# Solving the triangular inverse from the last row upwards, in a stick-breaking and RWKV-7 block on one core

## The chip, the core and the metric

The kernel runs on one core of a Trainium2 chip. Its metric is the device time of one execution in microseconds (us). Before the change the median of three runs is 1595.77 us (1595.27 to 1598.77). In this text PE is the matrix engine, PEld its weight loads, DVE the vector engine, ACT the scalar engine, POOL the general-purpose engine and SP the engine that issues the transfers.

## The reference

One block of a network on x of 1024 tokens by 1024 channels, float32: a normalised input projection, two parallel branches (causal stick-breaking attention with 8 heads, and RWKV-7 time mixing with 8 heads of 64 channels), a gated merge, an output projection and a gated feed-forward part. The change touches the RWKV-7 branch alone, whose core is a recurrence over the tokens:

```python
def step(state, inp):
    r_t, w_t, k_t, v_t, kk_t, a_t = inp
    sa = jnp.einsum('bhvk,bhk->bhv', state, -kk_t)
    state = (state * w_t[:, :, None, :]
             + sa[..., None] * (kk_t * a_t)[:, :, None, :]
             + v_t[..., None] * k_t[:, :, None, :])
    return state, jnp.einsum('bhvk,bhk->bhv', state, r_t)
```

The kernel computes it in chunks of 64 tokens. Within a chunk the steps depend on each other through a strictly triangular 64x64 matrix N per head and chunk, and the chunk's result needs the inverse of (I - N).

## The kernel before

**The order of the work.** The kernel first records every operation with its engine, and then a planner (`Block.schedule`, L413) puts all of them in an order: it simulates the engines with a cost for each operation (`cost`, L131), latencies between engines (L247) and a priority, and gives out the SBUF and PSUM places on the way. The operations are then issued in that order, so each engine works through a fixed queue. A recorded operation has the same line in the profile (L585), whoever recorded it; groups are told apart by the names of their tiles. The planner's price of a vector product depends on how its first operand is read: L155 gives `68 + 1.8 * n` ns if the last step of that operand is over 16 elements, and L157 gives `68 + 1.042 * n` otherwise, with n elements per partition.

**The stages.** Normalisation and small projections; the RWKV-7 branch (`rwkv`, L867); attention (L1130); merge; output projection; feed-forward. The RWKV-7 branch has four pairs of heads and two halves of the sequence, so eight units. A unit is one call of `rw_elementwise` (L896), which makes the chunk matrices `nx` (tile b_nx) and calls `rw_inverse` (L1024); afterwards `rw_chain` (L1075) carries the state through the eight chunks (tiles b_xv, b_sv) and `rw_post` finishes. Projections of the next pair and of the gates (tiles d_d, big_h) are recorded as fillers, which the planner lays between the steps of these units.

**The inverse.** A unit has 16 matrices of 64x64 (8 chunks by 2 heads). Each is cut in 32x32 blocks. Their two diagonal blocks are inverted by substitution on DVE, 32 blocks side by side; the block below is then made with two groups of small matmuls. The steps are:

1. `nd`: the diagonal blocks go to DRAM, and from there come back as `nl` (b_nl, L1029): 128 partitions, each with a whole 32x32 block, four partitions for one block. POOL writes the ones on the diagonal (L1030).
2. The substitution (L1035 to L1038): 31 steps, each of one product and one reduction. Step t multiplies column t of the block, read down the rows with a step of 32 elements, with the t+1 entries found so far of n rows of the inverse, and sums each product into one entry. The block is broadcast over the n rows.
3. Four stores to DRAM (`td`) and one load bring the inverse with its rows on partitions (`dt`, L1047). DVE transposes 32x32 blocks of it (`dn`, L1051).
4. `dn` is copied to `tt` by POOL (L1054) and is the right operand of the first group of small matmuls (`ph`, L1063); `dt` is the weight of the second (`pt`, L1069), which also needs two DVE copies of `ph`.

The tiles ts, tm, dt, dn and hb are all of the class q (four places), so they show as q_q.

Of the kernel before, what the change touches and what calls it, by code (L numbers as in the profile page):

```python
# [10 lines left out]
ALU = mybir.AluOpType  # L11
AX = mybir.AxisListType
# [3 lines left out]
P = 128  # L16
# [879 lines left out]
def rw_elementwise(b, u, p, hf, spill):  # L896
# [108 lines left out]
    with Offset(b, INV):  # L1005
        tt = rw_inverse(b, nd, nx, quads, tinit, p, hf)


        for g in range(2):
            pt = T("y", [P, 4, P])  # L1010
            cs = slice(4 * g, 4 * g + 4)
            with b.together():
                for c in range(4):
                    for h, rs in enumerate(halves):
                        nc.tensor.matmul(pt[rs, c, 0:CH], lhsT=tt[rs, 4 * g + c, :], rhs=bkt[rs, 4 * g + c, rs], start=True, stop=True)
                    for h, rs in enumerate(halves):
                        nc.tensor.matmul(pt[rs, c, CH:P], lhsT=tt[rs, 4 * g + c, :], rhs=nx[g][rs, c, 1, h, :], start=True, stop=True)
            for h, rs in enumerate(halves):
                nc.scalar.copy(bkt[rs, cs, rs], pt[rs, :, 0:CH])
                nc.scalar.copy(nx[g][rs, :, 1, h, :], pt[rs, :, CH:P])  # L1020
                nc.scalar.copy(nx[g][rs, :, 0, h, :], ar[rs, cs, 0:CH])


def rw_inverse(b, nd, nx, quads, tinit, p, hf):  # L1024

    nc = b.nc
    T = b.t
    nl = T("b", [P, 8 * P], F32, "nl")
    nc.sync.dma_start(nl[:], nd.rearrange("c a s t -> (c a) (s t)")[:, None, :].broadcast_to([32, 4, 1024]))  # L1029
    nc.gpsimd.memset(nl[:, 0:1024:33], 1.0)  # L1030
    nl = nl.rearrange("l (s t) -> l s t", s=32)
    ts = T("q", [P, 8, 32])
    nc.sync.dma_start(ts[:], tinit.rearrange("l (j t) -> l j t", j=8))
    tm = T("q", [P, 8, 32])
    for t in range(1, 32):  # L1035
        n = (t + 3) // 4
        nc.vector.tensor_tensor(out=tm[:, :n, : t + 1], in0=nl[:, None, 0 : t + 1, t].broadcast_to([P, n, t + 1]), in1=ts[:, :n, : t + 1], op=ALU.mult)
        nc.vector.tensor_reduce(out=ts[:, :n, t], in_=tm[:, :n, : t + 1], axis=AX.X, op=ALU.add)  # L1038
    td = b.scratch([32, 8, 4, 32], f"td{p}{hf}")
    stores = set()  # L1040
    for c in range(4):

        nc.sync.dma_start(td[:, :, c, :], ts[c:P:4])
        b.ops[-1].preds -= stores
        stores.add(b.ops[-1])
    dt = T("q", [P, 8, 32])
    nc.sync.dma_start(dt[:], td.rearrange("(c a) j k t -> (a j k) c t", a=4))  # L1047
    b.ops[-1].late = SHORT_RUNS

    dn = T("q", [P, 8, 32])  # L1050
    nc.vector.transpose(out=dn.rearrange("p c t -> p (c t)"), in_=dt.rearrange("p c t -> p (c t)"))  # L1051
    tt = T("b", [P, 8, CH], F32, "tt")
    for h, q, rs, qs in quads:
        nc.gpsimd.tensor_copy(tt[rs, :, qs], dn[rs])  # L1054
        if q == 0:
            nc.gpsimd.memset(tt[rs, :, 32:CH], 0.0)
    ph = T("y", [P, 8, 32])
    hb = T("q", [P, 8, 32])
    top = [slice(0, 32), slice(CH, CH + 32)]
    bot = [slice(32, CH), slice(CH + 32, P)]  # L1060
    with b.together():
        for c, h in ((c, h) for c in range(8) for h in range(2)):
            nc.tensor.matmul(ph[bot[h], c, :], lhsT=nx[c // 4][top[h], c % 4, 0, h, 32:CH], rhs=dn[top[h], c, :], start=True, stop=True)  # L1063
    for h in range(2):
        nc.vector.tensor_copy(hb[bot[h]], ph[bot[h]])
    pt = T("y", [P, 8, 32])
    with b.together():
        for c, h in ((c, h) for c in range(8) for h in range(2)):
            nc.tensor.matmul(pt[bot[h], c, :], lhsT=dt[bot[h], c, :], rhs=hb[bot[h], c, :], start=True, stop=True)  # L1069
    for h in range(2):  # L1070
        nc.scalar.copy(tt[bot[h], :, 0:32], pt[bot[h]])
    return tt
# [680 lines left out]
```

## Time and profile before

| what | value |
|---|---|
| median of the timed runs | 1595.77 us (1595.27 to 1598.77, 3 runs) |
| span of the profiled execution | 1597.4 us, 23915 instructions |
| DVE, ACT, POOL busy over the span | 1176.4, 733.4, 205.0 us |
| substitution's products and reductions | from 125.5 to 468 us, 248 of each |
| mean granted PE clock | 0.997 |
| transfers | 180.38 MB, mean 113 GB/s |

The profile records one execution. For each engine it lists when it worked, what it waited for when it did not, and in which queue position; the span is from the first instruction to the last. A row of a group gives the number of instructions, their total time in us and the mean of one in ns, and behind it how long the engine stood idle just before them.

### The profile page before, as it was taken

Reading aid. Unit: us, or ns where it says so; the run is one execution under the profiler, and the core shown is the slowest. Engines: PE = TensorE matmul, PEld = TensorE weight load, DVE = VectorE, ACT = ScalarE, POOL = GpSimd, SP = SyncE. Lnnn points to the kernel's source line nnn. Section 1 sums busy time; section 2 is a strip of 40 time slices with the busy share of each in tenths; the row PEclk is TensorE's granted clock in tenths of the full one; section 3 lists DMA queues with packets and bytes.
Section 4 is the critical chain, followed back from the end, with each engine's and each line's share of the span. In section 5 each row is a group of like instructions: output and inputs, shape, how many; then the busy total and the mean of one; then the engine's idle time right before and its main releaser. Section 6 shows DMA issues by size and latency. Waiting matters only on the chain.

```text
span 1597.4 us, 23915 instructions
## 1 busy us (share of the span) xinstructions
PE 1573.5 (99%) x8884; PEld 1275.1 (80%) x8884; DVE 1176.4 (74%) x2104; ACT 733.4 (46%) x1445; POOL 205.0 (13%) x383
## 2 busy tenths in 40 slices
PE   9999999999999999999999999999999999999998
PEld 7877877777778888888788888888888888888876
DVE  7568779878884888896269799766666666877585
ACT  7533334444345666675445664332332333454352
POOL 1031233433323232230000000000000000000000
PEclk9999999999999999999999999999999999999999
DMA  6523332342321000103643531232233233964445
GB/s 218 202 77 88 100 104 57 84 136 78 106 80 35 33 28 14 41 21 106 198 138 106 170 121 73 99 113 99 86 112 99 95 117 125 317 230 138 144 147 184
DMA packets 106822, 180.38 MB, mean 113 GB/s; under 512 B 42321, under 2 KB 43345, under 8 KB 106706
## 3 DMA queue, kind: packets, MB, share of 16 engines
q1 hardware_dynamic: 106706, 178.85, 34.3%
q8 instruction: 70, 1.15, 0.3%
q14 instruction: 46, 0.38, 0.1%
HBM read 129.27 MB, written 47.45 MB: 111 GB/s over the span
## 4 chain that ended last, share of the span: by engine, by line
PE 88%; DVE 6%; DMA 3%; ACT 1%; issue 1%; POOL 0%; SPq 0%; DVEq 0%; ACTq 0%; POOLq 0%
PE d_d L585 42%; PE e_e L585 19%; PE c_c L585 16%; PE y_y L585 12%; DVE q_q L585 1%; DMA b_wraw<-w_fd 1%; DVE big_h L585 0%; DVE b_nx L585 0%; DVE b_sv L585 0%; DVE b_xs L585 0%; DVE b_wraw L585 0%; DMA b_mg<-gsc 0%; DVE b_wd L585 0%; DMA b_tmp<-cum_d 0%; DMA g_d<-b_sg 0%
## 5 line engine op out<-in xcount | busy, mean ns | idle before, releaser
L585 PE MATMUL d_d<-big_h,whi_whi 128*128 128x512 f32 x1312 | 440.2, 408 | 1.6 <-ACT b_tmp L585 1.6
L585 PEld LDWEIGHTS d_d<-big_h,whi_whi 128*128 128x128 f32 x1312 | 240.7, 189 | 50.9 <-issue 5.0
L585 PE MATMUL d_d<-big_h,wlo_wlo 128*128 128x512 f32 x656 | 268.6, 410 | 0.0
L585 PEld LDWEIGHTS d_d<-big_h,wlo_wlo 128*128 128x128 f32 x656 | 123.9, 189 | 25.3 <-issue 2.9
L585 DVE TENSOR_TENSOR q_q<-b_nl,q_q 128x2 f32<-128x2 f32 (+30 forms) x248 | 88.3, 356 | 20.0 <-PE y_y L585 8.0
L585 ACT CAST whi_whi<-raw_raw 128x1024 fp32r<-128x1024 f32 (+1 forms) x58 | 53.7, 928 | 88.6 <-PE d_d L585 80.9
L585 DVE TENSOR_TENSOR_SCAN b_nb<-b_nb 128x128 f32<-128x128 f32 (+3 forms) x64 | 85.2, 1351 | 2.2 <-POOL b_nb L585 1.8
L585 DVE TENSOR_TENSOR wlo_wlo<-raw_raw,whi_whi 128x1024 fp32r<-128x1024 f32 (+1 forms) x58 | 63.3, 1092 | 26.1 <-ACT whi_whi L585 20.0
L585 POOL TENSOR_SCALAR sp_sp<-b_sv,pl_pl 64x64 f32<-64x64 f32 x120 | 61.3, 511 | 133.6 <-DVE b_sv L585 127.8
L585 ACT CAST b_wd<-b_wraw 128x512 fp32r<-128x512 f32 x70 | 42.3, 620 | 66.5 <-DVE b_wraw L585 31.5
L585 DVE TENSOR_REDUCE q_q<-q_q 128x1 f32<-128x2 f32 (+30 forms) x248 | 62.0, 250 | 6.8
L585 PE MATMUL e_e<-b_wd,big_act 128*128 128x512 f32 x264 | 66.5, 394 | 0.0
L585 PE MATMUL d_d<-b_wd,big_act 128*128 128x512 f32 x264 | 66.5, 394 | 0.0
L585 DVE TENSOR_TENSOR b_wd<-b_wraw,b_wd 128x512 fp32r<-128x512 f32 x70 | 46.5, 686 | 26.4 <-ACT b_wd L585 26.2
L585 PEld LDWEIGHTS e_e<-b_wd,big_act 128*128 128x128 f32 x264 | 49.6, 188 | 11.7
L585 PEld LDWEIGHTS d_d<-b_wd,big_act 128*128 128x128 f32 x264 | 49.6, 188 | 11.7
L585 POOL TENSOR_SCALAR_AFFINE_SELECT b_nb<-b_nb 128x128 f32<-128x128 f32 x64 | 40.1, 632 | 123.1 <-ACT b_nb L585 121.8
L585 DVE TENSOR_TENSOR b_wt<-c_c,b_wt 128x512 fp32r<-128x512 f32 (+2 forms) x96 | 50.4, 547 | 2.1 <-ACT b_wt L585 0.9
L585 PE MATMUL y_y<-b_wd,big_act 128*128 128x512 f32 x198 | 50.7, 394 | 0.9 <-DVE b_u L585 0.9
L585 PE MATMUL c_c<-b_wd,big_act 128*128 128x512 f32 x198 | 50.7, 394 | 0.2 <-DVE b_wd L585 0.2
L585 ACT COPY b_xv<-c_c 64x64 f32<-64x64 f32 x64 | 13.3, 208 | 79.0 <-PE c_c L585 44.4
L585 ACT CAST b_wt<-c_c 128x512 fp32r<-128x512 f32 (+2 forms) x96 | 43.6, 481 | 11.9 <-PE c_c L585 10.8
(635 smaller groups left out, 3536.0 us busy)
## 6 DMA issues: line engine op xcount, KB each, us to landing
raw_raw<-w_in SPq DMA_DIRECT2D x42, 512.0 KB, 3.6
act<-b_u SPq DMA_DIRECT2D x46, 256.0 KB, 2.3
raw_raw<-w_fg SPq DMA_DIRECT2D x22, 512.0 KB, 3.5
raw_raw<-w_fu SPq DMA_DIRECT2D x22, 512.0 KB, 3.6
b_wraw<-w_fd SPq DMA_DIRECT2D x22, 512.0 KB, 6.0
b_x<-x SPq DMA_DIRECT2D x16, 512.0 KB, 5.5
b_mg<-gsc SPq DMA_DIRECT2D x28, 256.0 KB, 5.4
raw_araw<-act SPq DMA_DIRECT2D x14, 512.0 KB, 6.3
```

Source lines behind the costliest of these rows:

```text
L585: getattr(getattr(self.real, op.engine), op.method)(**kw)
```

## The change

The substitution runs over rows instead of columns, from row 30 up to row 0. Row r of the inverse is found from row r of the block and from the rows below it that are already known, so each product reads the block along its row, with a step of one element. What the tile ts then holds is the transpose of what it held before. So the load from `td` now brings what was called `dn`, and DVE's transposition makes `dt` from it. The numbers of instructions and their sizes stay: a step r has 8-j rows of 32-r entries with j = (r+1)//4, the same sizes as before in the same order. The three-dimensional views now begin at column r of their 32-element rows.

```diff
-    for t in range(1, 32):
-        n = (t + 3) // 4
-        nc.vector.tensor_tensor(out=tm[:, :n, : t + 1], in0=nl[:, None, 0 : t + 1, t].broadcast_to([P, n, t + 1]), in1=ts[:, :n, : t + 1], op=ALU.mult)
-        nc.vector.tensor_reduce(out=ts[:, :n, t], in_=tm[:, :n, : t + 1], axis=AX.X, op=ALU.add)
+    for r in range(30, -1, -1):
+        j = (r + 1) // 4
+        nc.vector.tensor_tensor(out=tm[:, j:, r:], in0=nl[:, None, r, r:].broadcast_to([P, 8 - j, 32 - r]), in1=ts[:, j:, r:], op=ALU.mult)
+        nc.vector.tensor_reduce(out=ts[:, j:, r], in_=tm[:, j:, r:], axis=AX.X, op=ALU.add)
     td = b.scratch([32, 8, 4, 32], f"td{p}{hf}")
...
+    dn = T("q", [P, 8, 32])
+    nc.sync.dma_start(dn[:], td.rearrange("(c a) j k t -> (a j k) c t", a=4))
+    b.ops[-1].late = SHORT_RUNS
+
     dt = T("q", [P, 8, 32])
-    nc.sync.dma_start(dt[:], td.rearrange("(c a) j k t -> (a j k) c t", a=4))
-    b.ops[-1].late = SHORT_RUNS
-
-    dn = T("q", [P, 8, 32])
-    nc.vector.transpose(out=dn.rearrange("p c t -> p (c t)"), in_=dt.rearrange("p c t -> p (c t)"))
+    nc.vector.transpose(out=dt.rearrange("p c t -> p (c t)"), in_=dn.rearrange("p c t -> p (c t)"))
     tt = T("b", [P, 8, CH], F32, "tt")
     for h, q, rs, qs in quads:
         nc.gpsimd.tensor_copy(tt[rs, :, qs], dn[rs])
```

## The prediction

> **What bounds the kernel now.** I read the page's busy times first, then its chain of work.
>
> ```profile
> span 1597.4 us, 23915 instructions
> PE 1573.5 (99%) x8884; PEld 1275.1 (80%) x8884; DVE 1176.4 (74%) x2104; ACT 733.4 (46%) x1445; POOL 205.0 (13%) x383
> ...
> PE d_d L585 42%; PE e_e L585 19%; PE c_c L585 16%; PE y_y L585 12%; DVE q_q L585 1%; DMA b_wraw<-w_fd 1%; DVE big_h L585 0%; DVE b_nx L585 0%; DVE b_sv L585 0%; DVE b_xs L585 0%; DVE b_wraw L585 0%; DMA b_mg<-gsc 0%; DVE b_wd L585 0%; DMA b_tmp<-cum_d 0%; DMA g_d<-b_sg 0%
> ```
>
> PE has work 1573.5 of 1597.4 us, so 23.9 us is all that a better order of the other engines can win by removing PE's idle time. The substitution (DVE q_q) has 1% of the chain, 16 us. But a share of the chain isn't a gain: PE works beside most of these pieces, as the next view shows. It is the view of stretches, cut at my reading of the stages: normalisation and small projections, the RWKV-7 units, attention, merge, output and feed-forward. Behind the limits of each stretch stand its length, the busy times of PE, PEld, DVE, ACT and POOL, the granted clock and the transfers.
>
> ```profile
> 0.00:100.00 100.00, 95.77 (x508) 77.55 (x509) 59.79 (x73) 61.05 (x112) 14.22 (x43) 0.98 0.53 189
> 100.00:483.00 383.00, 373.94 (x3048) 294.28 (x3047) 313.98 (x845) 152.47 (x327) 119.85 (x231) 1.00 0.32 89
> 483.00:750.00 267.00, 266.08 (x1692) 225.99 (x1692) 210.99 (x304) 176.98 (x394) 70.93 (x111) 1.00 0.12 38
> 750.00:890.00 140.00, 138.34 (x597) 111.74 (x596) 91.77 (x149) 63.81 (x111) 0.00 (x0) 1.00 0.42 135
> 890.00:1597.00 707.00, 699.37 (x3046) 565.52 (x3044) 499.84 (x736) 279.09 (x503) 0.00 (x0) 1.00 0.41 139
> ```
>
> The substitution lies in the second stretch. There PE idles 383.0 - 373.9 = 9.1 us and DVE is busy 314.0 us, 82%. The first row is before the first substitution, so its 4.2 us stay. The rows after it hold 0.9, 1.7 and 7.6 us that the substitution doesn't cause. The waits of PE in the second stretch (total us, times, longest) say who ends most of the 9.1 us:
>
> ```profile
> PE e_e L585 <- DVE b_nx L585: 4.0, 3, 2.4
> PE d_d L585 <- ACT b_tmp L585: 1.6, 1, 1.6
> PE c_c L585 <- DVE b_sv L585: 1.5, 3, 0.8
> PE c_c L585 <- DVE b_xv L585: 0.4, 1, 0.4
> PE e_e L585 <- DVE b_tmp L585: 0.3, 1, 0.3
> ...
> PE y_y L585 <- DVE q_q L585: 0.2, 1, 0.2
> ```
>
> DVE ends 4.0 + 1.5 + 0.4 + 0.3 + 0.2 = 6.4 us. Only 0.2 us is for a result of the inverse (q_q); the rest is for other DVE work in whose queue the substitution's 496 instructions stand. So PE's own work is the bound, and what the substitution costs the kernel today is some part of these 6.4 us.
>
> **The change part by part.** *The products.* The group rows and the rows by shape, with count, total us and mean ns:
>
> ```profile
> L585 DVE TENSOR_TENSOR q_q<-b_nl,q_q 128x2 f32<-128x2 f32 (+30 forms) x248 | 88.3, 356 | 20.0 <-PE y_y L585 8.0
> L585 DVE TENSOR_REDUCE q_q<-q_q 128x1 f32<-128x2 f32 (+30 forms) x248 | 62.0, 250 | 6.8
> L585 DVE TENSOR_TENSOR q_q<-b_nl,q_q 128x240 f32<-128x240 f32 x8 | 4.7, 588 | 0.1
> L585 DVE TENSOR_TENSOR q_q<-b_nl,q_q 128x30 f32<-128x30 f32 x8 | 1.6, 205 | 0.2
> L585 DVE TENSOR_REDUCE q_q<-q_q 128x8 f32<-128x240 f32 x8 | 3.2, 405 | 0.2
> L585 DVE TENSOR_REDUCE q_q<-q_q 128x3 f32<-128x30 f32 x8 | 1.5, 186 | 0.3
> ```
>
> From 30 to 240 elements a product grows by (588 - 205) / 210 = 1.82 ns per element, and a reduction, which reads the same elements without the step of 32, by (405 - 186) / 210 = 1.04 ns. No row has a product of this kind with a step of one, so I bound it: at best it costs what the reduction costs, which takes 88.3 - 62.0 = 26.3 us from DVE; at worst nothing is won. Some of the 26.3 us isn't the step: it is waiting beside POOL, as the view in order of time shows for a product of five elements:
>
> ```profile
> 309.81 1.27 DVE L585 TENSOR_TENSOR q_q<-b_nl,q_q 128x5 f32<-128x5 f32 x1
> 309.79 1.27 POOL L585 TENSOR_TENSOR b_sh<-b_sh,b_tmp 128x512 f32<-128x512 f32 x1 [2.23 <-DVE q_q L585]
> 309.01 0.69 DVE L585 SCALAR_TENSOR_TENSOR b_ar<-b_sh,b_pp 128x512 f32<-128x512 f32 x1
> ```
>
> 1.27 us for 128x5 isn't its reading: it ends with POOL's product beside it (311.08 and 311.06), and a new order of reading doesn't cure that. I take the slopes: 0.78 ns less for each element. A unit's 31 products have 2928 elements (2, 3, 4, 5, 12 ... 240, 248, 256), so 2.3 us per unit, and 18.3 us for eight, out of DVE's 314.0. A loss from the products themselves I exclude by the last row just shown: b_ar reads b_pp, rows of 65 words that start at odd words every second time, much as the new views start at column r, and it takes 0.69 us for 512 elements, no more than its kind.
>
> [...]
>
> *What of it is on the path.* Nearly none, if the order stays. I went through PE's stalls and looked for long products just ahead in DVE's queue. The clearest is this:
>
> ```profile
> 391.12 0.59 DVE L585 TENSOR_TENSOR q_q<-b_nl,q_q 128x248 f32<-128x248 f32 x1
> 393.47 0.64 DVE L585 TENSOR_TENSOR q_q<-b_nl,q_q 128x256 f32<-128x256 f32 x1
> 398.46 1.28 DVE L585 TENSOR_TENSOR b_nx<-e_e,cst_cst 128x512 f32<-128x512 f32 x2
> 399.19 0.98 PE L585 MATMUL e_e<-b_ar,b_bk 64*128 64x128 f32 x4 [0.92 <-DVE b_nx L585]
> ```
>
> Two products of 248 and 256 elements come before the b_nx for which PE waited 0.92 us; each would be about 0.2 us shorter, so 0.4 us of this stall can go. The stalls on b_xv and b_sv have some 0.2 us of such products ahead, by the same slope. The biggest stall has only short ones:
>
> ```profile
> 125.28 0.15 POOL L585 MEMSET b_nl<- 128x32 f32 x1 [3.50 <-DMA nd<-b_nx]
> 125.47 0.16 DVE L585 TENSOR_TENSOR q_q<-b_nl,q_q 128x2 f32<-128x2 f32 x1 [2.77 <-POOL b_sh L585]
> ...
> 126.91 0.68 DVE L585 TENSOR_TENSOR b_nx<-e_e,cst_cst 128x512 f32<-128x512 f32 x1
> ...
> 127.64 0.60 PE L585 MATMUL e_e<-cst_cst,b_sg 128*128 128x128 f32 x3 [2.45 <-DVE b_nx L585]
> ```
>
> Here DVE stood 2.77 us at the head of its queue for the block's return from DRAM, then did eight instructions of 2 to 5 elements, then the b_nx that PE had awaited for 2.45 us. Contiguous reading does nothing for 5 elements. So 0.6 us in all.
>
> *The swap of dn and dt.* The same transfers and the same transposition move to other consumers:
>
> ```profile
> L585 DVE STREAM_TRANSPOSE q_q<-q_q 128x256 f32<-128x256 f32 x8 | 3.5, 443 | 2.2 <-DMA q_q<-td 2.2
> DMA to landing us min/median/max: 1.9/2.0/2.7
> ```
>
> POOL's copies and the first group of small matmuls no longer wait for the 443 ns transposition; the second group waits for it, behind PE's first group and two DVE copies that hide it. PE waited 0.2 us in all for q_q, so 0.2 us is the most that this wins. The second row is for all transfers through td, to landing. If the landing (2.0 us in the middle, 2.7 at most) were late against the plan, PE would now stand directly behind it, with the projections' matmuls queued behind PE, where DVE stood 2.2 us once; I keep that as a loss of at most 2.2 us and cost it at nothing, because even with the transposition in between PE stood only 0.2 us for this result. Nothing moves past a queue: SP issues the same four stores and one load per unit, and the tile classes have the same demand.
>
> *The new order.* The planner's price for these products falls (L155 to L157), by 0.758 ns times 2928, so 2.2 us per unit, and from the first substitution on it may lay all queues differently. PE's work stays the same; its 9.1 us of stalls are drawn anew, and with them one more cost. The view of stretches around the second stall (PE on ACT b_tmp, 1.6 us):
>
> ```profile
> 214.00:216.00 2.00, 1.38 (x34) 1.08 (x35) 0.17 (x2) 0.77 (x2) 0.00 (x0) 0.90 0.28 110
> 216.00:218.00 2.00, 2.00 (x5) 1.18 (x4) 1.94 (x5) 0.53 (x2) 0.00 (x0) 0.50 0.06 22
> 218.00:220.00 2.00, 2.00 (x34) 1.70 (x34) 1.65 (x4) 0.30 (x2) 0.00 (x0) 0.75 0.00 0
> ```
>
> PEclk falls to 0.90, 0.50 and 0.75: 2 x (0.10 + 0.50 + 0.25) = 1.7 us lost beyond the stall. The 2.45 us stall had no such row behind it. I bound the new order by 8.1 us gained (all 6.4 us on DVE, and this dip) and 4.2 us lost (below), and take zero, because PE is over 97% busy in this stretch and I see no row that pulls one way.
>
> *The sum.* -0.6 - 0.2 + 0 = -0.8 us. Taken from the profile's span, 1596.6 us; the span is 1.6 us over the median and inside the range of the three runs, and I give the forecast on the median: 1595.0 us.
>
> **The rivals.** *Faster: the relief reaches PE.* DVE has 18.3 us less to do in a stretch where it is 82% busy, and every stall on DVE is a matter of queue position. If new places in the queue clear half of the 6.4 us and the dip of the clock, 3.2 + 1.7 = 4.9 us go: 1590.9; all of it gives 1587.7. For it speaks that 6.4 of 9.1 us end with DVE; against it that the largest one comes from a transfer, and that the queue is planned, with any freed time given to the next planned work.
>
> *Slower: the block's return heads the queue.* With shorter products the planner may place the first products of a unit where the data is not back yet, as at 125.47, in front of DVE work that PE needs. It happened once in eight units with effect. Each further time costs 2.45 us, and with a dip of the clock 2.45 + 1.7 = 4.2 us: 1600.0. It decides from one such stall with a dip, or two without. Against it: the first substitution steps, whose place matters, are those whose price hardly changes.
>
> [...]
>
> *No effect of its own: the product isn't bound by reading.* If waiting beside POOL or fixed time hides the step of 32, products stay near 356 ns, and only the transposition's 0.2 us and no new order remain: 1595.6.
>
> **How the numbers follow.** A measurement of this kernel can tell about 0.2% from no change, 3.2 us: below 1592.6 is faster, above 1599.0 slower. The forecast has 0.39, and the rival of no effect 0.08; both lie within 0.2%, so 0.47 for the same. The faster rival has 0.32, since more of the stalls hang on DVE than on anything else; the slower one 0.21. The likeliest case's own range is 1592.6 to 1599.0. For 8 in 10 the range goes into both rivals: down to 1588.5, near their full 8.1 us, and up to 1600.0, one new stall with a dip; about 0.07 lies below and 0.11 above.
>
> **What would show it.** In the changed profile the group of products should fall from 356 to about 282 ns (88.3 - 18.3 = 70.0 us over 248), the row of 128x240 from 588 to near 405, the reductions stay at 250, and DVE's busy time in the second stretch fall to some 296 us, while PE's busy time stays. The transposition should come behind the first small matmuls or beside them. If PE's idle time in the stretch stays between 6 and 12 us, the forecast's mechanism holds. I am wrong if its idle time falls to 4 us or less (faster rival), if a wait of 2 us or more on b_nx behind a late b_nl, or a second row with PEclk 0.5, appears (slower rival), or if the time moves while PE's idle time does not.

## The result: 0.5% slower, with cheaper products

The changed kernel takes 1603.88 us (median of 5 runs, 1603.58 to 1606.3) against 1595.77 us before: the ratio is 1.0053, interval 1.0041 to 1.0065. The forecast was 1595.0 us with a range of 1588.5 to 1600.0, so the time lies 3.9 us above the range and on the other side of no change.

The span of this profile lies 1.8 us below the time of its own run (1602.1 for 1603.88 us), and so do the runs of the kernel before; its profile, with 1597.4 us, therefore belonged to a run of about 1599 us, slower than most: the two profiles differ by 4.7 us, the medians by 8.1. Where sizes matter below, I compare times, and profiles only for where the time goes; each kernel has one profiled execution.

The page of the changed kernel begins with:

```profile
span 1602.1 us, 23920 instructions
PE 1575.1 (98%) x8884; PEld 1273.6 (79%) x8884; DVE 1158.5 (72%) x2104; ACT 732.9 (46%) x1445; POOL 201.1 (13%) x383
```

The groups of the substitution, and the rows for 240 elements (count, total us, mean ns):

```profile
L585 DVE TENSOR_TENSOR q_q<-b_nl,q_q 128x2 f32<-128x2 f32 (+30 forms) x248 | 69.0, 278 | 13.4 <-POOL b_sh L585 2.5
L585 DVE TENSOR_REDUCE q_q<-q_q 128x1 f32<-128x2 f32 (+30 forms) x248 | 62.2, 251 | 7.1
L585 DVE TENSOR_TENSOR q_q<-b_nl,q_q 128x240 f32<-128x240 f32 x8 | 3.6, 446 | 0.2
L585 DVE TENSOR_REDUCE q_q<-q_q 128x8 f32<-128x240 f32 x8 | 3.2, 404 | 0.2
```

The products cost 69.0 us in place of 88.3, 278 ns each in place of 356: the change does on DVE what it says. The reductions stay. The same stretches as before (length, busy us of PE, PEld, DVE, ACT and POOL, granted clock, transfers):

```profile
100.00:483.00 383.00, 371.92 (x3156) 290.99 (x3156) 297.81 (x864) 154.47 (x339) 122.53 (x244) 1.00 0.31 87
483.00:750.00 267.00, 263.79 (x1553) 223.06 (x1552) 206.00 (x283) 171.78 (x377) 65.45 (x97) 1.00 0.12 38
750.00:890.00 140.00, 139.73 (x611) 112.98 (x610) 90.44 (x145) 63.39 (x110) 0.00 (x0) 1.00 0.43 139
...
```

DVE is busy 297.8 us in the RWKV-7 stretch, 16.2 less. But PE idles 383.0 - 371.9 = 11.1 us there, 2.0 more than before, and in the next stretch 267.0 - 263.8 = 3.2 us where it idled 0.9. So a lighter DVE came with longer stalls of PE. Who ends them, from 100 to 520 us, about the start of attention (total us, times, longest):

```profile
PE e_e L585 <- DVE b_nx L585: 6.0, 5, 2.4
PE c_c L585 <- DVE b_sv L585: 2.5, 5, 0.8
PE c_c L585 <- POOL b_pp L585: 1.6, 1, 1.6
PE d_d L585 <- DVE b_ql L585: 1.5, 1, 1.5
PE e_e L585 <- ACT b_qst L585: 0.8, 1, 0.8
```

The waits on b_nx grew from 4.0 to 6.0 us. Two of the five are long, 2.2 us at 127 us, the old one, and a new one. The view in order of time shows it (start, length, instruction, idle time before it and what ended it):

```profile
305.42 0.16 POOL L585 MEMSET b_nl<- 128x32 f32 x1 [5.22 <-DMA b_nl<-nd]
305.62 0.16 DVE L585 TENSOR_TENSOR q_q<-b_nl,q_q 128x2 f32<-128x2 f32 x1 [1.88 <-POOL b_nl L585]
...
307.37 0.69 DVE L585 TENSOR_TENSOR b_nx<-e_e,cst_cst 128x512 f32<-128x512 f32 x1
...
308.12 0.80 PE L585 MATMUL e_e<-cst_cst,b_pp 128*128 128x128 f32 x2 [2.42 <-DVE b_nx L585]
```

This is my slower rival to the letter: DVE stands 1.88 us at the head of its queue for the block's return from DRAM, does the first steps of the substitution, and only then the masking (the product with the triangular mask) into b_nx that PE has awaited for 2.42 us. And the granted clock falls (PEclk is the third number from the end):

```profile
306.00:308.00 2.00, 0.00 (x0) 0.00 (x0) 1.76 (x9) 0.48 (x1) 0.84 (x4) 0.95 0.00 0
308.00:310.00 2.00, 1.88 (x9) 1.88 (x10) 1.45 (x7) 0.00 (x0) 0.18 (x1) 0.50 0.15 24
310.00:312.00 2.00, 2.00 (x12) 1.91 (x12) 1.26 (x5) 1.17 (x4) 0.88 (x3) 0.69 0.06 9
```

2 x (0.05 + 0.50 + 0.31) = 1.7 us more. But the dip of the old order is gone in return, and 4.1 us would not explain 8.1. By the names of the tiles in the two traces, PE's first 732 matmuls stand in the old order and so do those behind the 4145th; between them 2931 of 3413 places hold another matmul. So the first question is what belongs to that order and what to the new form itself.

### The profile page after: what moved, and what is told of

The parts are those of the page before. It is cut to its first block, busy times and chain, and to the rows that moved or that the text cites. A ratio compares the mean times of both kernels' runs of the same rounds, so it can differ in the third digit from the quotient of the medians.

```text
span 1602.1 us, 23920 instructions
## 1 busy us (share of the span) xinstructions
PE 1575.1 (98%) x8884; PEld 1273.6 (79%) x8884; DVE 1158.5 (72%) x2104; ACT 732.9 (46%) x1445; POOL 201.1 (13%) x383
## 4 chain that ended last, share of the span: by engine, by line
PE 87%; DVE 6%; issue 2%; DMA 2%; ACT 1%; POOL 1%; SPq 0%; DVEq 0%; POOLq 0%; ACTq 0%
PE d_d L585 40%; PE e_e L585 19%; PE c_c L585 16%; PE y_y L585 12%; DVE q_q L585 2%; DMA b_nl<-nd 1%; DVE big_h L585 0%; DMA b_wraw<-w_fd 0%; DVE b_bk L585 0%; DVE b_nx L585 0%; DVE b_xs L585 0%; DVE b_sv L585 0%; DMA b_mg<-gsc 0%; DMA g_d<-b_sg 0%; DVE b_u L585 0%
## 5 line engine op out<-in xcount | busy, mean ns | idle before, releaser
L585 DVE TENSOR_TENSOR q_q<-b_nl,q_q 128x2 f32<-128x2 f32 (+30 forms) x248 | 69.0, 278 | 13.4 <-POOL b_sh L585 2.5
L585 DVE TENSOR_REDUCE q_q<-q_q 128x1 f32<-128x2 f32 (+30 forms) x248 | 62.2, 251 | 7.1
```

Of the source, the lines that this page charges most:

```text
L585: getattr(getattr(self.real, op.engine), op.method)(**kw)
```

## The experiments

All kernels compute the row form unless said otherwise. The theories at the start: O, the newly drawn order costs the time; P, the row form or the swap is slow on the chip.

**The new form in the old order.** The planner is given the old price of the products and the old dependences, and then gives every engine the queue of the kernel before.

```diff
+        b.ops[-1].cost = 68 + 1.8 * (8 - j) * (32 - r)
...
         nc.gpsimd.tensor_copy(tt[rs, :, qs], dn[rs])
+        swap(b.ops[-1], back, turn)
```

Here `back` is the load of dn, `turn` the transposition, and `swap` replaces the first by the second among the operations that the planner waits for; the same is done for the first small matmuls, and the reverse for the second.

> The changed kernel, but the planner sees the old price of the products (68 + 1.8 ns per element) and the old dependences (copies and first small matmuls behind the transposition), so that every engine's queue is that of the kernel before, instruction by instruction; only the reading along rows and the swap of dn and dt are new. Theory O (the 8 us come from the newly drawn order): 1595.0 us, my sum of -0.8 us on 1595.8, and the products at about 280 ns. Theory P (the row form itself or the swap is slow on the chip, for instance a wait on the landing): 1600 to 1604 us, with the loss at the same places in the queues.

Measured: 1593.24 us (12 runs) beside 1595.76 us of the kernel before, ratio 0.9984 (0.9974 to 0.9993). Theory O holds and P falls: the new form in the old places is 2.5 us *faster*. The step from this order to the changed kernel's own costs 1603.88 - 1593.24 = 10.6 us. Its products and its waits:

```profile
L585 DVE TENSOR_TENSOR q_q<-b_nl,q_q 128x2 f32<-128x2 f32 (+30 forms) x248 | 70.9, 286 | 20.1 <-PE y_y L585 9.0
```

```profile
PE e_e L585 <- DVE b_nx L585: 3.0, 3, 1.6
PE d_d L585 <- ACT b_tmp L585: 1.6, 1, 1.6
PE c_c L585 <- DVE b_sv L585: 1.2, 2, 0.8
```

The waits on b_nx are 3.0 us where the profile before has 4.0, but that doesn't show what the cheaper products won: 0.8 us of it lies at 127 us (2.45 to 1.65 us), behind products of 2 to 5 elements, where POOL, and DVE behind it, stood 0.8 us less for the block (3.50 to 2.71 us), and the stall behind the two long products, from which I had taken 0.4 us, went only from 0.92 to 0.79 us. Two stretches that together hold the same work, cut at the first matmul of attention's values and at the first one of the merge's second part, show what the new order loses; first the old order, then the changed kernel (length, PE busy, instructions):

```profile
100.00:519.70 419.70, 412.14 (x3400) 1.00 0.30 85
519.70:805.20 285.50, 285.14 (x1594) 1.00 0.20 64
```

```profile
100.00:522.20 422.20, 408.55 (x3373) 1.00 0.30 84
522.20:814.50 292.30, 291.39 (x1621) 1.00 0.19 63
```

The same work takes 705.2 us and 714.5. PE idles 419.7 - 412.1 + 285.5 - 285.1 = 7.9 us in the old order, and 422.2 - 408.6 + 292.3 - 291.4 = 14.6 us in the new one. So of the 9.3 us between them, 6.6 are idle time, and 2.7 are in PE's busy time for the same matmuls. The clock doesn't account for these 2.7: each of the two profiles has one dip of 1.7 us there; what does stays open. (27 matmuls have moved from the first stretch to the second, which is part of why the second is longer.) The spans differ by 1.9 us more, in work where PE's order is the same in both.

**The new order with the old reading.** The same queues as the changed kernel, the price held, but the products go down the columns. They then read the block's other half, so this kernel doesn't make the inverse; the numbers and sizes of its instructions are the same:

```diff
-in0=nl[:, None, r, r:].broadcast_to([P, 8 - j, 32 - r])
+in0=nl[:, None, r:, r].broadcast_to([P, 8 - j, 32 - r])
```

> The changed kernel in its own order, with the planner's price held as it is, but the products read the block down its columns again with a step of 32 elements, so the block's lower half is read and the inverse it makes is another one; the numbers and sizes of instructions are the same. Products back near 356 ns. Theory O: the time stays with the order, 1603.9 to about 1606 us, at most the 18 us of DVE work partly showing. Theory P with the reading as the cause: back to about 1596 us.

Measured: 1617.5 us, ratio 1.0127 (1.011 to 1.0143). That is 11.5 us beyond the range of theory O and further from that of P; of the two, only O has the time stay with the order, and what it missed is how much the order depends on the short products.

```profile
L585 DVE TENSOR_TENSOR q_q<-b_nl,q_q 128x2 f32<-128x2 f32 (+30 forms) x248 | 85.1, 343 | 12.9 <-POOL b_sh L585 2.2
```

In the new order 16.1 us more of products (85.1 - 69.0) cost 13.6 us of time; in the old order 17.4 us more (88.3 - 70.9) cost 2.5, the swap included. So the new order isn't only another one: it has hardly any slack on DVE. That the planner, believing the products cheap, filled their place would explain it.

**Price and swap apart.** Two orders between the two: the old price with the new dependences, and the new price with the old ones.

> The changed kernel with the old price of the products in the planner, and the new dependences of the swap: a third order. Theory O: another draw, somewhere within about 8 us of 1596 to 1604 us, products at about 280 ns. If the fall of the price alone makes the new order bad, about 1595.5 us; if the swap's dependences do, about 1604 us.

> The changed kernel with the new price of the products, while the planner sees the old dependences (copies and first small matmuls behind the transposition): a fourth order. Theory O: another draw within the same 8 us. If the price alone makes the order bad, about 1604 us; if the swap's dependences do, about 1595.5 us.

Measured: 1597.43 us (ratio 1.0014, 0.9999 to 1.0029) and 1599.76 us (1.0025, 1.0016 to 1.0035). Neither alone does it: from 1593.2 us, the new dependences cost 4.2, the new price 6.5, both 10.6. So 4 of the 10.6 us come without any change of the price, as far as one order of each kind can show it.

**The first steps put behind b_nx.** In the changed kernel's own order, and in the old one, two maskings into b_nx each are issued ahead of the first steps of a substitution that stood in front of them; the rest of the queues stays. The core of the edit, on the finished list:

```python
late = [op for op in dve[at : at + 18] if op in masked]
end = dve.index(late[1])
move = [op for op in dve[at:end] if op in steps]
rest = [op for op in order if op not in move]
k = rest.index(late[1]) + 1
order = rest[:k] + move + rest[k:]
```

> The changed kernel in its own order but for two places on DVE: where the first steps of a substitution stand ahead of the two maskings into b_nx (at about 125 and 306 us), these maskings now come first; all other work of all engines keeps its order. Theory Q (the first steps head DVE's queue, wait for the block's return and hold up b_nx): PE's waits of 2.2 and 2.4 us on b_nx go, and the half-clock row behind 308 us with them, so 4 to 6 us less: 1598 to 1600 us. Theory R (these waits are cover for work that is late anyway): less than 1.5 us, 1602.5 or more.

> The row form in the order of the kernel before, with the same move at the two places where this order has first steps ahead of b_nx (one of them the stall of 1.65 us at about 127 us). Theory Q: 1 to 2 us less than the 1593.2 us of that order, 1591 to 1592 us. Theory R: 1593.2 us.

Measured: 1599.13 us in the new order (ratio 1.0022, 1.0013 to 1.0032, where it was 1.0053), 4.8 us less for two moves, as theory Q had it. The waits and the clock of this kernel at the same place, and the two stretches as above:

```profile
PE c_c L585 <- DVE b_sv L585: 4.5, 6, 1.6
PE d_d L585 <- DVE b_ql L585: 1.5, 1, 1.5
PE e_e L585 <- DVE b_nx L585: 1.4, 3, 0.9
```

```profile
306.00:308.00 2.00, 1.26 (x7) 1.09 (x8) 1.86 (x8) 0.24 (x2) 1.06 (x3) 1.00 0.35 60
308.00:310.00 2.00, 2.00 (x14) 1.72 (x13) 1.74 (x9) 1.50 (x3) 0.78 (x2) 1.00 0.19 33
310.00:312.00 2.00, 2.00 (x11) 1.52 (x10) 1.77 (x10) 0.21 (x1) 0.10 (x1) 1.00 0.94 251
...
100.00:518.50 418.50, 406.99 (x3373) 1.00 0.30 85
518.50:811.40 292.90, 291.34 (x1621) 1.00 0.19 63
```

b_nx is down from 6.0 to 1.4 us and the clock stays whole, but much of it comes back, above all as waits on b_sv (2.5 to 4.5 us): PE's idle time over the two stretches falls only from 14.6 to 418.5 - 407.0 + 292.9 - 291.3 = 13.1 us. The stretches are 3.1 us shorter, 1.5 of them idle time, and the rest about the dip of 1.7 us. The other 2.3 us between the two spans (1602.1 and 1596.7) lie behind the stretches, in work that the move doesn't touch. So the profiles show about 3 of the 4.8 us as the moves' own. In the old order theory R holds: the same move gave nothing, 1593.54 us beside 1593.24. Its stall of 1.65 us went, but another, of 2.04 us on b_sv, came elsewhere. A stall that is taken away needn't count: here other work was late behind it.

**Draw or price.** Is a cheap price bad in itself (theory S), or is every order a draw (theory L)? Six more prices, with the new dependences; only the figure that the planner uses is changed:

```diff
+        b.ops[-1].cost = 68 + 1.4 * (8 - j) * (32 - r)
```

> The changed kernel with the planner's price of a product raised by 1 ns (69 + 1.042 ns per element), a change too small to mean anything, which still gives a PE order that differs in part. Theory L (an order is a draw; small causes move it by microseconds): anywhere from 1596 to 1606 us, clearly off 1603.9 by more than 1 us more likely than not. Theory S (the cheap price is what makes orders bad, since it leaves DVE no slack): 1603 to 1605 us.

> The changed kernel with the planner's price of a product at 68 + 2.4 ns per element, 1.4 ns per element more than it costs. Theory S (slack in the plan helps): at or below the 1597.4 us of the price with 1.8. Theory L: a draw, from 1593 to 1604 us.

> The changed kernel with the planner's price of a product lowered by 2 ns (66 + 1.042 ns per element); nearly all of PE's order after the first substitution differs. Theory S (cheap prices make bad orders): 1602 to 1607 us, like the two cheap orders before. Theory L (a draw): as likely below 1600 us as above.

> The changed kernel with the planner's price of a product at 68 + 1.4 ns per element. Theory S: between the cheap orders and the 1597.4 us of 1.8, 1598 to 1602 us. Theory L: a draw from 1593 to 1605 us.

> The changed kernel with the planner's price of a product at 68 + 2.0 ns per element. Theory S: 1594 to 1598 us, between the orders of 1.8 (1597.4) and 2.4 (1595.3). Theory L: a draw from 1593 to 1605 us.

> The changed kernel with the planner's price of a product at 68 + 3.0 ns per element, three times the slope that it has. Theory S: 1593 to 1597 us, unless the inverse now comes too late for its unit. Theory L: a draw from 1593 to 1605 us.

| planner's price of a product, ns | time, us | ratio to before (interval) | PE idle, us | PE on b_nx, us |
|---|---|---|---|---|
| 66 + 1.042 n | 1601.06 | 1.0036 (1.0024 to 1.0048) | 13.1 | 4.6 |
| 68 + 1.042 n (the changed kernel) | 1603.88 | 1.0053 (1.0041 to 1.0065) | 14.6 | 6.0 |
| 69 + 1.042 n | 1604.76 | 1.0056 (1.0041 to 1.0072) | 15.7 | 3.1 |
| 68 + 1.4 n | 1597.72 | 1.0013 (1.0003 to 1.0023) | 11.3 | 3.3 |
| 68 + 1.8 n | 1597.43 | 1.0014 (0.9999 to 1.0029) | 12.9 | 2.8 |
| 68 + 2.0 n | 1596.16 | 1.0001 (0.9991 to 1.001) | 8.7 | 2.7 |
| 68 + 2.4 n | 1595.32 | 1.0002 (0.9991 to 1.0012) | 11.0 | 3.0 |
| 68 + 3.0 n | 1602.65 | 1.0041 (1.0026 to 1.0056) | 15.4 | 3.1 |

The last two columns come from the profiles: PE's idle time over the same work as above, from 100 us to the merge's second part, and its waits on b_nx up to attention.

The three cheap prices give the three slowest orders up to 2.4 ns, as S has it. But they aren't three independent draws: by the names of the tiles, PE's order at 69 differs from that of the changed kernel in only 517 of 8884 places, and at 66 in 1284 (its expectation took nearly all behind the first substitution to differ), where it differs from the order before the change in 2931. So S is favoured and not proven. Two expectations of it missed: 66 + 1.042 n came out 1 us below its range, 1.4 slightly below too, and at 3.0 the time jumps up again by 7 us, which S allowed only with an excuse. There is a draw in it as well: the three cheap prices, 1 or 2 ns apart, lie up to 3.7 us apart.

The columns from the profiles say something more. PE's idle time goes broadly with the time: the four orders over 1600 us have 13.1 us or more of it, the other four 12.9 or less. The waits on b_nx don't: the slowest order of the table has 3.1 us of them, like the fast ones, and the new price with the old dependences (1599.76 us) has 2.5. So the stall at 306 us is part of the changed kernel's loss, and not what makes slow orders slow in general.

**The planned return of the block.** Why should the true price be bad? One candidate had shown itself: the planner takes the block back from DRAM sooner than it is. It plans 3.6 us from the start of the load to POOL's ones on the diagonal (524288 bytes at 360 a ns, L170, and 2060 ns with a margin of 80, L252). At 306 us in the changed kernel the load starts here:

```profile
299.60 0.57 SPq L585 DMA_DIRECT2D b_nl<-nd  x1
```

POOL, which by its row in the section on the result waits for this load, begins at 305.42 us, 5.8 us after it, where 3.6 were planned. The two last kernels keep the true price and give the load of `nl` a later planned landing, by 1 and by 2 us:

```diff
     nc.sync.dma_start(nl[:], nd.rearrange("c a s t -> (c a) (s t)")[:, None, :].broadcast_to([32, 4, 1024]))
+    b.ops[-1].late = 2000.0
```

> The changed kernel at its own price of the products, but the planner takes the block (b_nl) to be back from DRAM 1 us later than before. If the planned return is the cause: no wait of 2 us on b_nx behind the first steps, and 1595 to 1599 us. If any lateness matters and only a dear price covers it: 1601 us or more. Theory L: a draw from 1593 to 1605 us.

> The same with a return 2 us later, about what DVE stood waiting ahead of the first steps at 125 and 306 us (2.5 and 1.9 us). If the planned return is the cause: 1595 to 1599 us, both stalls of over 2 us on b_nx gone. If only a dear price covers lateness: 1601 us or more.

Measured: 1599.43 us (ratio 1.0022, 1.001 to 1.0034) and 1596.68 us (1.0008, 0.9998 to 1.0017). With 2 us more, 7.2 of the 10.6 us are back at the true price. The longest waits of PE in that kernel, up to attention:

```profile
PE c_c L585 <- DVE b_xv L585: 1.7, 4, 0.6
PE y_y L585 <- DMA q_q<-td: 1.5, 2, 1.4
PE c_c L585 <- DVE b_sv L585: 1.2, 2, 0.6
```

No wait on b_nx of any weight is left, and PE's idle time over the same work is 10.6 us with 1 us more and 9.3 with 2, where the changed kernel has 14.6; the 1.5 us on td are PE standing directly behind a landing, the small loss that I had kept at up to 2.2 us for the swap. The first run, 0.4 us over its range, is a near miss of the expectation. These are new orders too, so a lucky draw can't be excluded; but they were aimed at the cause, and both came out below all three orders of the cheap prices. That is evidence for the planned return, and not proof.

No version beats the row form in the old order, 1593.24 us, 0.16% under the kernel before. That leaves a rival which no run tests: of the twelve orders that were planned here, the old one is the best, and if it was a lucky one, or kept because it was good, part of the 10.6 us is the loss of leaving it, whatever the price.

## Why the prediction was wrong, point by point

- **The products.** 18.3 us less on DVE and 282 ns each were forecast; the changed kernel shows 88.3 - 69.0 = 19.3 us and 278 ns. The rival of no effect of its own falls. (The 16 us of the chain that I gave the substitution are the page's rounded 1%; the chain's own view has 1.4%, 22 us, and no term rests on it.) The row of 240 elements came to 446 ns in the changed kernel and not near the reduction's 404; in the old order it is 400 ns by the rows of that profile:

```profile
L585 DVE TENSOR_TENSOR q_q<-b_nl,q_q 128x240 f32<-128x240 f32 x8 | 3.2, 400 | 0.1
```

- **Odd words.** That the new views start at column r, an odd one in 15 of 31 steps, was to cost nothing; what I had for it was one row, b_ar's, with runs of 64 words (0.69 us for 512 elements). The reductions read such views too, in runs of 2 to 32 words, and cost 62.2 us after 62.0: the traces show no loss in the short runs either.
- **What lies on the path.** -0.6 us for the products and -0.2 for the swap were forecast at fixed order. Measured there: -2.5 us (by the interval, -1.1 to -4.1). The sign was right and the size too small. Where the rest was won the two profiles don't show, and the 0.4 us that I had placed at one stall came to 0.13.
- **The swap.** I cost it at -0.2 us and wrote that nothing moves past a queue. Its dependences alone gave a new order that is 4.2 us slower than the old one, with the price unchanged. At its place it did what I expected: the transposition was to run beside the first small matmuls, and does, in the changed kernel's first unit:

```profile
158.41 0.69 PE L585 MATMUL y_y<-q_q,b_nx 32*32 32x32 f32 x32
158.42 0.43 DVE L585 STREAM_TRANSPOSE q_q<-q_q 128x256 f32<-128x256 f32 x1
```

- **The new order: the step that failed.** I wrote that I "take zero, because PE is over 97% busy in this stretch and I see no row that pulls one way", and bounded the loss by one stall with a dip of the clock, 4.2 us. It was 10.6 us, and in the profiles PE idles 14.6 us in place of 7.9 over the same work. A row that may pull one way stood in my own text: DVE idle 2.77 us at the head of its queue, for a block that the planner believed to be there. A plan that is wrong about a landing can get worse when the work behind that landing is planned shorter, because more is packed against the same error. This is my reading: the last two runs are in line with it, but it doesn't cover the 4.2 us of the dependences, and of the 6.6 us that PE idles more, only 2.9 stand directly behind a late block (2.17 and 2.42 us, where the old order has 1.65). And I had put the slower rival low with "the first substitution steps, whose place matters, are those whose price hardly changes": their price hardly changes, but their place does, since it hangs on all that is planned before them.
- **The slower rival** named one part of the loss and its price: one place more was found at 306 us, with a stall of 2.42 us and a dip of 1.7, 4.1 us where I had said 4.2. It came once, as I had priced it. What I got wrong is that it would be all: the other 6.5 of the 10.6 us, or more, since the old order has a dip of its own, are many smaller waits (on b_sv, b_pp, b_ql and others) and PE's longer busy time, and I can't put them down place by place.
- **The signs.** PE's idle time of 11.1 us lies between the 6 and 12 us that were to show that the forecast's mechanism holds, while a wait of over 2 us on b_nx behind a late block, the sign against it, had come too. The first sign was too wide, and it was read in a stretch cut by time: 2.3 us more of idleness lay in the next one.
- **The time of before** was set by the median and not by the profile's span, which was right. The dip of the clock that I read there stands in the profile of the row form in the old order too.

## What to carry to other kernels

Where a planner lays the queues, a cheaper instruction is two changes: what it costs on the chip, and what the plan does with the price; a changed dependence is a third. Measure them apart, by giving the planner the old price and the old dependences. When the plan's times are off somewhere (a landing, or a product that ends only with POOL's beside it, as the 1.27 us for five elements at 309.81 us did before), a too dear price elsewhere may have been the slack that hid it; before the true price goes in, look in the profile for engines that idle at the head of their queue with ready work behind, and mend that time first. And judge a new order by PE's idle time over the same work, not by the one wait that stands out.

## What was not expected of the hardware

In the changed kernel, PE's clock fell to 0.50 behind an idle time of 2.42 us, as it did before behind 1.61 us, but not behind the 2.17 us at 127 us. Each such dip cost about 1.7 us, and in the profile with the first steps behind two maskings 0.95, 0.50 and 0.69 became 1.00 in all three rows. The same idle time doesn't always bring a dip: at about 34 us, where all sixteen kernels still have the same order, PE idles 2.0 to 2.1 us in every profile, and the clock falls to about half behind it in twelve (0.50 to 0.56 in the lowest row) and stays whole in four, both kernels with the later return among these. So a dip in one execution belongs in part to chance; what decides it, no run here tests.
